# Other sums for feed forward's seven products, other places for the last parts of the output projection, and own banks for transposes in a two-layer decoder kernel

## The chip, the core and the metric

The kernel runs on one core of a Trainium2 chip. The core has five engines with an instruction queue each: TensorE (PE in the profile, with its weight loads as PEld), VectorE (DVE), ScalarE (ACT), GpSimd (POOL) and SyncE (SP), which issues the DMAs here. The metric is the device time of one execution in microseconds (us). Data lies in SBUF; PE writes into eight PSUM banks, each of which holds a 128x512 float32 tile.

## What is computed

Two layers, each with three kinds of attention beside each other and a feed forward part, on 1024 tokens of 1024 columns. The change touches the end of the output projection and the feed forward part:

```
for layer in range(DEPTH):            # DEPTH = 2
    ...                               # h = rmsnorm(x, ln1_g), three mixers
    mixed = jnp.concatenate([out_a, out_b, out_c], axis=-1)
    x = x + mixed @ w_o[layer]
    u = rmsnorm(x, ln2_g[layer]) @ w_up[layer]          # 1024 -> 4096
    x = x + jnp.square(jax.nn.relu(u)) @ w_down[layer]  # 4096 -> 1024
return rmsnorm(x, final_g)
```

## The kernel before

Every product of 128x128 by 128x512 is three matmuls: each operand is split into a high part, rounded to PE's format, and a low part, the remainder; high by high, high by low and low by high are summed in one bank (`mm3`, line 500). So each operand costs a rounding (`copy` with the kind "fhi", on ACT or POOL) and a subtraction (`pair` with "flo", on DVE or POOL).

The two matrices of feed forward are multiplied by a scheme of seven products instead of eight: tokens, inner columns and outer columns are each halved, and each of the seven products takes a sum or difference of quarters from the left and one from the right. Before, the tables `left` and `right` (line 1313 on) hold these sums, five of the seven a side being real ones (`parts`, line 1320); each product's result is then added to several quarters of the output.

Up (1024 to 4096) runs over 16 pairs `p` of column blocks. `up_a` (line 1435) does products 4 and 2, which need the first half of the tokens alone; `up_b_` (line 1447) the other five. `up_load` fetches the weights `wu`, `up_parts` makes the weights' sums `s_wu` and their high and low parts `uh`, `ul` in 16 slots of the tag "w". A pair uses four banks (products 4 and 2 share one, 5 and 3, 1 and 7, and 6); ACT copies a bank's first result away (`fsnap`) before the second product is added to it. `relu2` makes the squared ReLU. The quarters and their sums `hc` go to DRAM for down. Five pairs' `up_a` run ahead (`AHEAD`).

The normed tokens come from four steps `tp` of two token tiles each: ACT squares a tile with a sum (`jk_u`), DVE takes the root by Newton steps (`rv`, `ra`, `usq`), ACT and POOL scale the tile (`fnorm`), PE transposes it into a bank (`ptu`, from the same eight-deep tag "u" that up's products use), and ACT and DVE bring it to SBUF with the gain (`xq`). `x_parts` makes the tokens' sums `s_x` and their parts `xc`.

Down (4096 to 1024) runs in four blocks of pairs (`BLOCKS`), in each over the seven products in `ORDER` and four token tiles. `ha` are the parts of the tokens' side, `hb` of the weights'; results go to five accumulators `acc` and to the residual `xd`, and after the last block 32 additions a layer combine the accumulators into the residual. The last pair is done plainly (`pdl`, with `hpa` and `hpb`).

The output projection adds four groups of two column blocks to x (`project`, line 1193). The last two groups, (2, 3) and (4, 5), run after attention; the last one's parts are popped from the list `bl`, four at each step `tp`.

All operations are first recorded and then issued in an order that a planner works out: it walks over all engines with a table of costs and hops, takes on each engine the ready operation with the lowest rank (program position plus `nc.bias`), and picks the engine where `WAYS` leaves a choice. Each engine then runs its row strictly in that order. All instructions carry the line of the helper that issues them (L416), so places are told by tiles.

## Time and profile before

| | |
|---|---|
| time, median of 3 runs | 2592.06 us (2591.5 to 2594.74) |
| the profiled execution | 2590.82 us, span 2589.0 us |
| mean granted clock of PE | 0.983 of full speed |
| PE busy | 2479.6 us (96%), 12808 matmuls and transposes |
| DVE, ACT, POOL busy | 2146.6 (83%), 1265.7 (49%), 935.9 us (36%) |
| DMA | 360.61 MB, mean 139 GB/s |

PE's busy time is a share of a span that has very different stages; a busy PE may also run at half its clock. So the stages are read apart, by the table of stretches, which gives busy time, number of instructions, granted clock and DMA share of each. In the first layer the feed forward part starts near 622 us, up's steady pace is between 740 and 960, down ends near 1300; in the second the same places lie near 1903, 2020 to 2240 and 2560.

### The profile page before, as it was taken

To read this page: it belongs to the slowest core of one execution; us is meant where nothing else is said; L and a number is where in the kernel's file an instruction comes from. 1 tells how busy PE (TensorE), PEld (TensorE's weight loads), DVE (VectorE), ACT (ScalarE), POOL (GpSimd) and SP (SyncE) were. 2 spreads that over 40 slices of the span, in tenths; PEclk is the share of its full clock that TensorE was granted. 3 is DMA by queue.
4 is the path that set the end of the run, shared out by engine and by line. 5 is a ranking of instruction groups with operands and counts; after the bars stand their busy time and mean duration, and the time that the engine had idled before them with its cause. 6 is when DMAs were issued, how large, how long until landed. Compare 5 with 4: busy or idle time off the path is not lost.

```text
span 2589.0 us, 39628 instructions
## 1 busy us (share of the span) xinstructions
PE 2479.6 (96%) x12808; PEld 2085.7 (81%) x12808; DVE 2146.6 (83%) x4489; ACT 1265.7 (49%) x2626; POOL 935.9 (36%) x1093
## 2 busy tenths in 40 slices
PE   9999999998899999999899999999979999999996
PEld 7777889987688878888688778898867888788884
DVE  4688988888888778899856799978889887789999
ACT  3566667734544444233235666777255444442332
POOL 1344355644100013336624344557431000133374
PEclk9999999999999999999999999999989999999998
DMA  8355434523344467444353454344324454765332
GB/s 253 100 133 137 122 83 108 149 76 122 97 164 162 155 213 262 130 148 122 122 164 98 131 137 118 82 115 142 93 85 141 148 179 137 279 199 162 119 98 85
DMA packets 292639, 360.61 MB, mean 139 GB/s; under 512 B 48848, under 2 KB 172112, under 8 KB 292432
## 3 DMA queue, kind: packets, MB, share of 16 engines
q1 hardware_dynamic: 292432, 358.08, 45.0%
q8 instruction: 102, 1.67, 0.3%
q14 instruction: 105, 0.86, 0.1%
HBM read 231.63 MB, written 94.90 MB: 126 GB/s over the span
## 4 chain that ended last, share of the span: by engine, by line
PE 74%; DVE 13%; DMA 5%; issue 3%; ACT 2%; POOL 2%; SPq 1%; DVEq 0%; POOLq 0%; ACTq 0%
PE pu L416 21%; PE pd L416 16%; PE po L416 5%; PE pf_C L416 5%; PE pf_A L416 4%; PE s_B L416 3%; PE pj L416 2%; PE o_B L416 2%; PE o_A L416 2%; DVE hb L416 2%; PE ptp_A L416 2%; PE ptp_B L416 2%; PE s_A L416 2%; DVE xd L416 1%; DVE p_C L416 1%
## 5 line engine op out<-in xcount | busy, mean ns | idle before, releaser
L416 PE MATMUL pd<-hb,ha 128*128 128x512 f32 x2520 | 578.7, 391 | 7.6 <-DVE hb L416 5.7
L416 PEld LDWEIGHTS pd<-hb,ha 128*128 128x128 f32 x2520 | 474.2, 189 | 111.1 <-DVE hb L416 9.7
L416 PE MATMUL pu<-xc,uh 128*128 128x512 f32 x1792 | 550.8, 391 | 6.5 <-ACT s L416 3.4
L416 PEld LDWEIGHTS pu<-xc,uh 128*128 128x128 f32 x1792 | 334.3, 188 | 83.8 <-ACT s L416 10.9
L416 PE MATMUL pu<-xc,ul 128*128 128x512 f32 x896 | 344.3, 390 | 0.8 <-DVE ul L416 0.8
L416 ACT ACTIVATE hb<-s_wd 128x512 fp32r<-128x512 f32 x135 | 83.9, 628 | 241.4 <-DVE s_wd L416 112.6
L416 PEld LDWEIGHTS pu<-xc,ul 128*128 128x128 f32 x896 | 168.2, 188 | 37.2 <-DVE ul L416 1.7
L416 DVE TENSOR_TENSOR ha<-hr,ha 128x512 fp32r<-128x512 f32 x164 | 148.0, 905 | 38.7 <-POOL ha L416 30.2
L416 ACT ACTIVATE uh<-s_wu 128x512 fp32r<-128x512 f32 x124 | 77.6, 631 | 204.1 <-PE pu L416 172.4
L416 POOL TENSOR_SCALAR ha<-hr 128x512 fp32r<-128x512 f32 x88 | 76.3, 870 | 228.7 <-DVE acc L416 89.3
L416 POOL TENSOR_SCALAR uh<-s_wu 128x512 fp32r<-128x512 f32 x36 | 31.0, 862 | 323.6 <-DVE ul L416 191.2
L416 DVE TENSOR_TENSOR ul<-s_wu,uh 128x512 fp32r<-128x512 f32 x160 | 109.9, 690 | 42.8 <-ACT uh L416 42.2
L416 DVE TENSOR_TENSOR hb<-s_wd,hb 128x512 fp32r<-128x512 f32 x135 | 136.9, 1030 | 0.8 <-ACT hb L416 0.6
L416 ACT ACTIVATE p_C<-p_C,w_C 128x256 f32<-128x256 f32 (+7 forms) x128 | 98.9, 773 | 54.3 <-DVE w_C L416 53.7
L416 DVE TENSOR_TENSOR s_wu<-wu,wu 128x512 f32<-128x512 f32 x160 | 108.9, 692 | 13.9 <-DMA wu<-in_w_up_dram 8.2
L416 POOL TENSOR_SCALAR p_A<-p_A,w_A 128x128 f32<-128x128 f32 (+3 forms) x96 | 76.9, 803 | 116.6 <-DVE w_A L416 83.3
L416 DVE TENSOR_TENSOR xr<-po,xr 128x512 f32<-128x512 f32 x128 | 86.5, 683 | 31.8 <-PE po L416 31.4
L416 DVE TENSOR_TENSOR s_wd<-wd,wd 128x512 f32<-128x512 f32 x142 | 100.8, 740 | 7.3 <-DMA wd<-in_w_down_dram 7.3
L416 PE MATMUL pf_C<-wh_C,hh 128*128 128x512 f32 x256 | 104.5, 412 | 1.3 <-ACT cqj L416 0.9
L416 PE MATMUL pf_C<-wl_C,hh 128*128 128x512 f32 x256 | 104.3, 407 | 1.3 <-DVE wl_C L416 1.0
L416 PE MATMUL po<-h_wo,mixh 128*128 128x512 f32 x256 | 102.9, 402 | 0.1
L416 PE MATMUL pf_A<-wh_A,hh 128*128 128x512 f32 (+1 forms) x256 | 100.1, 395 | 2.7 <-POOL wh_A L416 1.6
(344 smaller groups left out, 6771.4 us busy)
## 6 DMA issues: line engine op xcount, KB each, us to landing
hr<-hc_dram SPq DMA_DIRECT2D x210, 256.0 KB, 2.8
hc_dram<-hc SPq DMA_DIRECT2D x150, 256.0 KB, 3.0
...
wd<-in_w_down_dram SPq DMA_DIRECT2D x120, 256.0 KB, 4.6
...
```

The costliest lines, as they stand in the source:

```text
L416: getattr(getattr(self.nc, eng), method)(*[real(v) for v in args], **{k: real(v) for k, v in kw.items()})
```

## The change

The four parts of the change in words:

- Feed forward takes another form of the seven products, with four sums a side, where each sum is built on the one before. In up, products 1 and 2 share a bank, 5 and 3 share one, 6, 7 and 4 a third; what stands in a bank is added by DVE to the outputs before the next product goes into the same bank. In down the products run in the order 6, 5, 7, 4, 3, 1, 2; three accumulators stay, products 7, 4, 3 and 2 are added straight to the residual, and the combination (20 additions a layer) follows product 1 of the last block.
- The output projection's last group has three column blocks and one: tokens 0 to 511 get three blocks into eight banks and then the last one; the rest follows tile by tile between the norms (`project_rest`).
- The transposes have a tag of banks of their own ("t", four deep).
- The second half of the tokens goes from PSUM straight into the sums (`xt`), the first half through `xq` as before.

Its core:

```diff
-BANKS = {'s': 6, 'pt': 3, 'o': 2, 'x': 3, 'c': 6, 'l': 4, 'v': 3, 'f': 5, 'j': 8, 'u': 8, 'd': 8}
+BANKS = {'s': 6, 'pt': 3, 'o': 2, 'x': 3, 'c': 6, 'l': 4, 'v': 3, 'f': 5, 'j': 8, 'u': 8, 't': 4, 'd': 8}
...
-ORDER = (5, 4, 3, 2, 1, 6, 7)
+ORDER = (6, 5, 7, 4, 3, 1, 2)
...
-XB = (150, 100, -40)
+XB = -40
 NB = (0, 0)
-XR = 4
+XR = 1
...
-        groups = [(6, 0), (7, 1), (2, 3), (4, 5)]
+        groups = [(6, 0), (7, 1), (2, 3, 4), (5,)]
...
+        most, last = project_load(2), project_load(3)
+        po_ = {}
+        for t in range(4):
+            for c in range(2):
+                po_[t, c] = bank("d", f"po_{L}_2_{t}_{c}")
+                project_mm(po_[t, c], t, c, *most, True, False)
+        for t in range(4):
+            for c in range(2):
+                project_mm(po_[t, c], t, c, *last, False, True)
+                project_add(po_[t, c], t, c)
+        def project_rest(t):
+            for c in range(2):
+                o = bank("d", f"po_{L}_2_{t}_{c}")
+                project_mm(o, t, c, *most, True, False)
+                project_mm(o, t, c, *last, False, True)
+                project_add(o, t, c)
...
+        def up_sum(p, i, a, b, op):
+            v = tl("tmp", [P, 4, P], f"su_{L}_{p}_{i}")
+            pair("fadd", v, a, b, op)
+            return v
...
+            if tp > 1:
+                project_rest(2 * tp)
+                project_rest(2 * tp + 1)
...
-                pt = bank("u", f"ptu_{L}_{tp}_{k}")
+                pt = bank("t", f"ptu_{L}_{tp}_{k}")
...
+                    for d in range(2):
+                        copy("fevac", xq[k][d][:, cs], p_[d], g_[d])
+                    for d in range(2):
+                        x_parts(1 + d, k, cs, xq[k][d][:, cs])
+                else:
+                    q = tl("tmp", [P, 2, 256], f"xt_{L}_{tp}_{k}")
+                    r = tl("tmp", [P, 256], f"xt2_{L}_{tp}_{k}")
+                    b11, b21 = [xq[k][d][:, cs] for d in range(2)]
+                    nc.vector.scalar_tensor_tensor(q[:, 0], p_[0], g_[0], b11, ALU.mult, ALU.subtract)
+                    b22 = x_tile_of(3, k)
+                    nc.scalar.activation(b22[:, 0, cs], p_[1], AF.Copy, scale=g_[1])
+                    nc.vector.scalar_tensor_tensor(b22[:, 1, cs], p_[1], g_[1], b22[:, 0, cs].bitcast(F32), ALU.mult, ALU.subtract)
+                    x_parts(5, k, cs, q[:, 0])
+                    nc.vector.scalar_tensor_tensor(r, p_[1], g_[1], q[:, 0], ALU.mult, ALU.subtract)
+                    x_parts(6, k, cs, r)
+                    pair("fadd", q[:, 1], r, b11, ALU.subtract)
+                    x_parts(7, k, cs, q[:, 1])
+                    pair("fadd", r, b21, r, ALU.subtract)
+                    x_parts(4, k, cs, r)
...
+        def plus(o, ps, v):
+            nc.vector.tensor_tensor(out=o, in0=ps, in1=v, op=ALU.add)
...
         def up_a(p):
...
+                up_load(p, (0,) if p < AHEAD else (0, 1))
+            for d in range(2):
+                up_parts(p, 1 + d, up_w[p, 0, d])
+            o = bank("u", f"pu_{L}_{p}_1")
+            up_mm(p, 1, o, True)
+            copy("fsnap", e[:, 0], o)
+            up_mm(p, 2, o, False)
+            relu2(e[:, 1], o)
...
+            a11, a12, a21, a22 = [up_w[p, f, d] for f in range(2) for d in range(2)]
+            s1 = up_sum(p, 1, a21, a22, ALU.add)
+            up_parts(p, 5, s1)
+            s2 = up_sum(p, 2, s1, a11, ALU.subtract)
+            up_parts(p, 6, s2)
+            pair("fadd", s2, a12, s2, ALU.subtract)
+            up_parts(p, 3, s2)
+            s3 = up_sum(p, 3, a11, a21, ALU.subtract)
+            up_parts(p, 7, s3)
+            up_parts(p, 4, a22)
+            h12, h22 = [tl("pp", [P, 512], f"h{z}_{L}_{p}") for z in (12, 22)]
+            z_ = bank("u", f"pu_{L}_{p}_5")
+            up_mm(p, 5, z_, True)
+            plus(h22, z_, m1)
+            up_mm(p, 3, z_, False)
+            plus(h12, z_, m1)
+            y = bank("u", f"pu_{L}_{p}_6")
+            up_mm(p, 6, y, True)
+            plus(h12, y, h12)
+            relu2(h12, h12)
+            up_mm(p, 7, y, False)
+            plus(h22, y, h22)
+            relu2(h22, h22)
+            up_mm(p, 4, y, False)
+            plus(m1, y, m1)
+            relu2(m1, m1)
...
+            pair("fadd", c1, b21, b22, ALU.add)
+            keep(5, c1)
+            pair("fadd", c2, c1, b11, ALU.subtract)
+            keep(6, c2)
+            pair("fadd", c3, b11, b21, ALU.subtract)
+            keep(7, c3)
+            c4 = tl("pp", [P, 512], f"hc_{L}_{p}_3")
+            pair("fadd", c4, b12, c2, ALU.subtract)
+            keep(3, c4)
...
+        acc = {i: [tl("stk", [P, 2, 512], f"acc_{L}_{i}_{h}") for h in range(2)] for i in (6, 5, 1)}
...
+                    if i == 6:
+                        dn_t[p] = tl(TT[p - b0], [P, 2, 512], f"wt_{L}_{p}")
+                    if i in (4, 5, 6, 7):
+                        t3, t2 = dn_t[p][:, 0], dn_t[p][:, 1]
+                    if i == 6:
+                        pair("fadd", t3, b22, b12, ALU.subtract)
+                        pair("fadd", t2, t3, b11, ALU.add)
+                    if i == 4:
+                        pair("fadd", t2, b21, t2, ALU.subtract)
+                    t1 = None
+                    if i == 5:
+                        t1 = tl("tmp", [P, 512], f"wt1_{L}_{p}")
+                        pair("fadd", t1, b12, b11, ALU.subtract)
+                    hi_lo(b[:, 0], b[:, 1], {1: b11, 2: b21, 3: b22, 5: t1}[i] if i in (1, 2, 3, 5) else t3 if i == 7 else t2)
...
+                    if i in (6, 5, 1):
+                        to = acc[i][t // 2][:, t % 2]
                     else:
-                        to = acc[i][t // 2][:, t % 2]
-                    if first and i < 6:
+                        to = {7: xs[t + 4][:, 512:], 4: xs[t + 4][:, 0:512], 3: xs[t][:, 512:], 2: xs[t][:, 0:512]}[i]
+                    if first and i in (6, 5, 1):
                         copy("fsnap", to, o)
                     else:
-                        nc.vector.tensor_tensor(out=to, in0=o, in1=to, op=ALU.add)
+                        plus(to, o, to)
+                    if b1 == BLOCKS[-1] and i == 1:
+                        a6, a5, a1 = [acc[z][t // 2][:, t % 2] for z in (6, 5, 1)]
+                        pair("fadd", xs[t + 4][:, 0:512], xs[t + 4][:, 0:512], a1, ALU.add)
+                        pair("fadd", a5, a5, a1, ALU.add)
+                        pair("fadd", xs[t + 4][:, 512:], xs[t + 4][:, 512:], a5, ALU.add)
+                        pair("fadd", a1, a1, a6, ALU.add)
+                        pair("fadd", xs[t][:, 512:], xs[t][:, 512:], a1, ALU.add)
```

What it moves is shown at three places; `before` has L416 and the change L418 in its rows, and the last number of a name tells copies of a tile apart.

PE's row in layer 1 from the last parts of the output projection (`po`) to up's first products (`pu`), before; `ptu_1` is the transposes of step 1, `pu_0_4` product 4 of pair 0:

```order
L416 MATMUL po_3_4_0_8073<-h_wo_5_0_7869,mixl_5_7886 128x512
L416 MATMUL ptu_0_0_8082<-ident,xr_0_6513 128x128 x4
...
L416 MATMUL ptu_0_3_8103<-ident,xr_0_6513 128x128 x4
L416 MATMUL po_3_4_1_8111<-h_wo_4_1_7835,mixh_4_7807 128x512
...
L416 MATMUL po_3_7_1_8228<-h_wo_5_1_7888,mixl_5_7886 128x512
L416 MATMUL ptu_1_0_8267<-ident,xr_0_6513 128x128
...
L416 MATMUL ptu_1_3_8289<-ident,xr_3_6805 128x128
L416 MATMUL ptu_2_0_8296<-ident,xr_3_6805 128x128
...
L416 MATMUL ptu_2_3_8307<-ident,xr_3_6805 128x128 x3
L416 MATMUL ptu_3_0_8417<-ident,xr_6_5223 128x128
...
L416 MATMUL ptu_3_3_8441<-ident,xr_7_5231 128x128
L416 MATMUL pu_0_4_8449<-xc_4_0_8123,uh_0_4_7947 128x512 x2
```

The same place after the change:

```order
L418 MATMUL po_2_4_1_7994<-h_wo_3_1_7619,mixl_3_7803 128x512
L418 MATMUL ptu_0_0_8002<-ident,xr_0_6505 128x128 x4
...
L418 MATMUL ptu_1_3_8119<-ident,xr_3_6775 128x128
L418 MATMUL po_2_5_1_8090<-h_wo_3_1_7619,mixl_3_7803 128x512
...
L418 MATMUL po_2_7_0_8194<-h_wo_5_0_7854,mixl_5_7852 128x512
L418 MATMUL ptu_2_0_8221<-ident,xr_3_6775 128x128
...
L418 MATMUL po_2_7_1_8236<-h_wo_5_1_7869,mixl_5_7852 128x512
L418 MATMUL pu_0_1_8287<-xc_1_0_8027,uh_0_1_8200 128x512 x2
...
L418 MATMUL pu_4_1_8476<-xc_1_0_8027,uh_4_1_8339 128x512
L418 MATMUL ptu_3_0_8505<-ident,xr_6_5223 128x128
...
L418 MATMUL pu_4_1_8476<-xc_2_3_8071,ul_4_2_8375 128x512
L418 MATMUL pu_0_5_8647<-xc_5_0_8277,uh_0_5_8641 128x512 x2
```

Steps 1, 2 and 3 stood together behind the last `po`; now `po` matmuls stand ahead of steps 0 to 2, and the products of up that need only the first tokens ahead of step 3.

PE's row in up at pair 8, before, from product 5 to product 3 in the bank `pu_8_5`:

```order
L416 MATMUL pu_8_5_9992<-xc_5_3_8359,ul_8_5_9859 128x512
L416 MATMUL pu_8_1_10045<-xc_1_0_8381,uh_8_1_9904 128x512 x2
L416 MATMUL pu_8_1_10045<-xc_1_0_8381,ul_8_1_9911 128x512
L416 MATMUL pu_8_1_10045<-xc_1_1_8386,uh_8_1_9904 128x512 x2
L416 MATMUL pu_8_1_10045<-xc_1_1_8386,ul_8_1_9911 128x512
L416 MATMUL pu_8_5_9992<-xc_3_0_8630,uh_8_3_9870 128x512 x2
```

After the change, from product 5 to 3, and around product 7 in the bank `pu_8_6`:

```order
L418 MATMUL pu_8_5_9877<-xc_5_3_8451,ul_8_5_9724 128x512
L418 MATMUL pu_8_6_9901<-xc_6_8314,uh_8_6_9734 128x512 x2
L418 MATMUL pu_8_6_9901<-xc_6_8314,ul_8_6_9744 128x512
L418 MATMUL pu_8_6_9901<-xc_6_8314,uh_8_6_9734 128x512 x2
L418 MATMUL pu_8_5_9877<-xc_3_0_8275,uh_8_3_9764 128x512 x2
...
L418 MATMUL pu_10_1_9941<-xc_1_2_8058,uh_10_1_9823 128x512
L418 MATMUL pu_8_6_9901<-xc_7_8332,uh_8_7_9777 128x512 x2
...
L418 MATMUL pu_8_6_9901<-xc_7_3_8535,ul_8_7_9789 128x512
L418 MATMUL pu_10_1_9941<-xc_1_2_8058,uh_10_1_9823 128x512
L418 MATMUL pu_10_1_9941<-xc_1_2_8058,ul_10_1_9836 128x512
L418 MATMUL pu_10_1_9941<-xc_1_3_8068,uh_10_1_9823 128x512 x2
L418 MATMUL pu_10_1_9941<-xc_1_3_8068,ul_10_1_9836 128x512
L418 MATMUL pu_8_6_9901<-xc_4_0_8361,uh_8_4_9812 128x512 x2
```

DVE's row there, with the additions that read the banks between the products:

```order
L418 TENSOR_TENSOR h_0_8_9903<-pu_8_5_9877,ua_8_9643 128x512
L418 TENSOR_TENSOR ul_9_6_9908<-su_9_2_9781,uh_9_6_9899 128x512
L418 TENSOR_TENSOR su_9_2_9781<-wu_9_1_0_9603,su_9_2_9781 128x512
L418 TENSOR_TENSOR h_0_8_9929<-pu_8_5_9877,ua_8_9643 128x512
L418 TENSOR_TENSOR ul_9_3_9934<-su_9_2_9781,uh_9_3_9926 128x512
L418 TENSOR_TENSOR su_10_2_9943<-su_10_1_9891,wu_10_0_0_9651 128x512
L418 TENSOR_TENSOR h_0_8_9929<-pu_8_6_9901,h_0_8_9929 128x512
L418 TENSOR_TENSOR ul_9_7_9951<-su_9_3_9795,uh_9_7_9939 128x512
L418 TENSOR_TENSOR su_10_3_9957<-wu_10_0_0_9651,wu_10_0_1_9656 128x512
L418 TENSOR_TENSOR h_0_8_9903<-pu_8_6_9901,h_0_8_9903 128x512
```

Between two products in one bank five matmuls of the other bank or of pair 10 stand now, and the reader is a DVE addition (`h_0_8<-pu_8_5`) among sums and low parts; before, six stood there and ACT read the bank.

POOL's row at the end of down in layer 1, before; `xd` is the residual, `acc_3_0` an accumulator's tile:

```order
L416 TENSOR_TENSOR hb_14_2_13544<-wd_14_0_0_13136,hb_14_2_13544 128x512
L416 TENSOR_TENSOR s_wd_14_1_13572<-wd_14_0_0_13136,wd_14_1_1_13152 128x512
L416 TENSOR_TENSOR xd_0_11270<-xd_0_11270,acc_3_0_11586 128x512 x2
L416 TENSOR_TENSOR acc_4_1_11514<-acc_4_1_11514,acc_5_1_11398 128x512
L416 TENSOR_TENSOR hb_14_1_13617<-s_wd_14_1_13572,hb_14_1_13617 128x512
L416 TENSOR_TENSOR s_wd_12_6_13644<-wd_12_0_0_12381,wd_12_0_1_12385 128x512
L416 TENSOR_TENSOR xd_3_11352<-xd_3_11352,acc_2_0_11672 128x512
L416 TENSOR_TENSOR acc_3_0_11586<-acc_3_0_11586,acc_2_0_11672 128x512
L416 TENSOR_TENSOR xd_3_11352<-xd_3_11352,acc_2_0_11672 128x512
```

And after the change, from the last tokens' parts on:

```order
L418 TENSOR_SCALAR ha_13_2_13444<-hr_13_2_13348 128x512
L418 TENSOR_SCALAR hpa_30_13465<-hpr_30_0_13392 128x512
L418 TENSOR_TENSOR acc_1_0_11642<-acc_1_0_11642,acc_6_0_11213 128x512
L418 TENSOR_SCALAR wh_0_13506<-wr_0_13481,g_518 128x512
L418 TENSOR_TENSOR hpb_30_13515<-hpr_30_0_13392,hpa_30_13465 128x512
L418 TENSOR_TENSOR hpb_31_13527<-hpr_31_0_13428,hpa_31_13517 128x512
L418 TENSOR_TENSOR hpb_30_13515<-hpr_30_1_13415,hpa_30_13465 128x512
L418 TENSOR_TENSOR hpb_31_13527<-hpr_31_1_13460,hpa_31_13517 128x512
L418 TENSOR_TENSOR acc_1_1_11683<-acc_1_1_11683,acc_6_1_11226 128x512 x2
```

The additions that combine accumulators stood in a row on POOL; now three are left there, and the low parts `hpb` of the last pair, which were DVE's, stand between them.

## Rows read from the trace of the kernel before

**Rows 1.** The page: busy time of each engine, its share of the span, instructions.

```profile
PE 2479.6 (96%) x12808; PEld 2085.7 (81%) x12808; DVE 2146.6 (83%) x4489; ACT 1265.7 (49%) x2626; POOL 935.9 (36%) x1093
```

**Rows 2.** Stretches (us from the span's start): length, busy time (instructions), clock, DMA.

```profile
622.00:660.00 38.00, 22.05 (x109) 19.38 (x109) 31.03 (x97) 25.02 (x54) 18.47 (x26) 0.73 0.20 77
660.00:700.00 40.00, 38.13 (x166) 30.67 (x165) 34.92 (x64) 25.69 (x52) 6.34 (x8) 1.00 0.32 93
740.00:960.00 220.00, 218.78 (x961) 179.26 (x960) 179.03 (x279) 102.84 (x182) 18.34 (x22) 1.00 0.50 167
960.00:985.00 25.00, 24.55 (x107) 19.67 (x106) 16.33 (x26) 8.57 (x16) 4.97 (x6) 1.00 1.00 366
1220.00:1270.00 50.00, 42.37 (x176) 33.57 (x174) 48.99 (x51) 11.72 (x21) 47.30 (x29) 0.97 0.23 69
1270.00:1302.00 32.00, 29.78 (x153) 25.41 (x153) 24.98 (x39) 14.42 (x28) 6.01 (x7) 0.89 0.67 237
1903.00:1940.00 37.00, 21.07 (x104) 18.49 (x103) 30.38 (x97) 24.86 (x53) 18.28 (x26) 0.72 0.19 75
2500.00:2550.00 50.00, 41.34 (x172) 32.73 (x170) 49.04 (x52) 11.72 (x21) 45.07 (x28) 0.94 0.19 58
1272.00:1278.00 6.00, 5.78 (x15) 4.55 (x16) 5.48 (x10) 0.73 (x1) 1.57 (x2) 0.54 0.71 187
```

**Rows 3.** Chain that ended last: start, length in us, instructions without a wait.

```profile
983.55 181.71 PE pd L416 x799
1295.16 7.10 PE ptx L416 x64
```

**Rows 4.** In order of time, projection's end, layer 1: start, length; brackets: idle, releaser.

```profile
614.79 0.39 PE L416 MATMUL po<-h_wo,mixl 128*128 128x512 f32 x1
615.22 0.69 DVE L416 TENSOR_TENSOR xr<-po,xr 128x512 f32<-128x512 f32 x1 [0.63 <-PE po L416]
621.82 2.08 PE L416 MATMUL ptu<-ident,xr 128*128 128x128 f32 x16
637.44 6.21 PE L416 MATMUL ptu<-ident,xr 128*128 128x128 f32 x32 [4.00 <-POOL xr L416]
654.93 0.47 PE L416 MATMUL ptu<-ident,xr 128*128 128x128 f32 x1 [11.28 <-ACT xr L416]
```

**Rows 5.** In order of time at the end of down, layer 1, DVE and PE.

```profile
1271.48 0.68 DVE L416 TENSOR_TENSOR hpb<-hpr,hpa 128x512 fp32r<-128x512 f32 x1
1272.22 0.80 PE L416 MATMUL pdl<-h_wd,hpb 128*128 128x512 f32 x1 [6.34 <-DVE hpb L416]
```

**Rows 6.** Groups of DVE, 640 to 740: busy us, mean ns, idle before.

```profile
L416 DVE TENSOR_TENSOR xc<-s_x,xc 128x256 fp32r<-128x256 f32 x22 | 10.6, 510 | 1.6 <-ACT xc L416 1.1 <-POOL xc L416 0.3
L416 DVE TENSOR_TENSOR s_x<-xq,xq 128x256 f32<-128x256 f32 x19 | 7.3, 416 | 0.0
L416 DVE TENSOR_SCALAR xq<-ptu,g 128x256 f32<-128x256 f32 x9 | 4.0, 479 | 4.1 <-PE ptu L416 4.1
```

**Rows 7.** Groups of POOL and DVE in down's last block, 1210 to 1270.

```profile
L416 POOL TENSOR_TENSOR xd<-xd,acc 128x512 f32<-128x512 f32 x11 | 18.5, 1698 | 0.0
L416 POOL TENSOR_TENSOR acc<-acc,acc 128x512 f32<-128x512 f32 x11 | 17.7, 1616 | 1.9 <-DVE acc L416 1.8
L416 DVE TENSOR_TENSOR ha<-hr,ha 128x512 fp32r<-128x512 f32 x13 | 15.9, 1230 | 0.0
L416 DVE TENSOR_TENSOR hb<-s_wd,hb 128x512 fp32r<-128x512 f32 x10 | 14.4, 1442 | 0.0
L416 DVE TENSOR_TENSOR acc<-pd,acc 128x512 f32<-128x512 f32 x17 | 11.5, 680 | 0.9 <-PE pd L416 0.9
```

**Rows 8.** Groups of PE and ACT, 740 to 960, then DVE's wait there (total, times, longest).

```profile
L416 PE MATMUL pu<-xc,uh 128*128 128x512 f32 x641 | 196.8, 390 | 1.2 <-ACT s L416 1.2
L416 ACT ACTIVATE s<-pu 128x512 f32<-128x512 f32 x24 | 14.0, 585 | 5.7 <-DMA hc_dram<-hc 2.3 <-DVE hc L416 1.6 <-DVE ul L416 1.0
DVE ul L416 <- ACT uh L416: 18.2, 15, 2.6
```

More of the change, by code (lines that the diff above doesn't have):

```diff
@@ new lines, in project_mm, with project_add @@
+        def project_mm(o, t, c, ws, mx, start, stop):
+            ts_ = slice(t * P, (t + 1) * P)
+            for fi in range(len(mx)):
+                mm3(o, mx[fi][0][:, ts_], mx[fi][1][:, ts_], ws[fi][c][0], ws[fi][c][1], start and fi == 0, stop and fi == len(mx) - 1)
+        def project_add(o, t, c):
+            cs = slice(c * 512, (c + 1) * 512)
+            nc.vector.tensor_tensor(out=xs[t][:, cs], in0=o, in1=xs[t][:, cs], op=ALU.add)
+        def project(gi):
+            box = []
+            def part(t, c):
+                o = bank("f", f"po_{L}_{gi}_{t}_{c}")
+                project_mm(o, t, c, *box[0], True, True)
+                project_add(o, t, c)
+            return [(0, lambda: box.append(project_load(gi)))] + [(1296, lambda t=t, c=c: part(t, c)) for t in range(NT) for c in range(2)]
@@ L1408, in tile_trunk, with up_mm @@
[L1408 to L1424 removed]
+        def up_mm(p, i, o, start):
+            wh, wl = up_h[p, i]
+            for k in range(4):
+                mm3(o, wh[:, k], wl[:, k], xc[i, k][:, 0], xc[i, k][:, 1], start and k == 0, k == 3)
@@ L1465, in up_b_ @@
[L1465 to L1480 removed]
+                up_load(p, (0, 1))
@@ L1513, in dn_load @@
                     dn_w[p, f, z] = q
+        TT = ("stk", "stk", "stk", "hs")
         for b0, b1 in zip(BLOCKS, BLOCKS[1:]):
+            dn_t = {}
             for p in range(b0, b1):
```

241 lines of the change are left out of this document (81 added, 160 removed).

## The prediction, made before the changed kernel ran

> **What bounds the kernel now.** I read the engines' busy times first: TensorE (PE) is busy for 2479.6 of 2589.0 us [rows 1], so no engine has to get faster; some 109 us of idle PE, and the time at a low granted clock, are all that can be won. Next I read the stretches [rows 2] against a pitch. In a long chain without waits 799 matmuls of 128x512 take 181.71 us, 0.2275 each; 64 transposes take 7.10, 0.111 each [rows 3]. With these, a stretch's loss is its length less its PE instructions at those prices:
> - 622 to 660 (end of output projection, norms, start of up): 64 transposes (7.1), 45 matmuls (10.2), so 38.0 - 17.3 = 20.7 lost, at clock 0.73. Then 660 to 700: 40 - 166 x 0.2275 = 2.2. Layer 2 has the same place at 1903: 104 instructions, about 20.8 lost.
> - 740 to 960 (up at its steady pace): 220 - 961 x 0.2275 = 1.4, clock 1.00.
> - 1220 to 1270 (last block of down): 50 - 176 x 0.2275 = 10.0; 1270 to 1302 loses 4.6 more (64 transposes, 89 matmuls), 2500 to 2550 in layer 2 10.9.
> So three places a layer matter. Last I read those in order of time. At the first [rows 4] PE does its 42 remaining projection matmuls, then has nothing but 48 transposes: it waits 4.00 us for x normed by GpSimd (POOL) and 11.28 us for ScalarE (ACT), because each pair of tiles needs its square, a Newton root and a scaling one after another; the second transposes run slowly, 32 in 6.21 us. At the end of down PE waits 6.34 us for `hpb` [rows 5], a VectorE (DVE) subtraction queued behind the final combination.
>
> **The change part by part.** PE's work is equal: as many matmuls and transposes, same shapes. So each term is a change of loss.
>
> *Output projection's last parts.* The merged groups give tokens 0 to 511 first; 24 short matmuls finish them, and what remains for tokens 512 to 1023 (96 matmuls, 21.8 us, against 42 before) stands between the transposes. Let T0 be the end of those 24. From the start of a tile's second addition to the first transpose the chain of before took 621.82 - 615.22 = 6.6 us [rows 4]. Tile 1's second addition starts at about T0 - 2.5, so `ptu_0` can start at T0 + 4.1; PE comes to it after 18 matmuls, T0 + 4.1. `ptu_1` follows 16 transposes (1.8) and 23 matmuls (5.2) later, T0 + 11.1; its chain, behind the first on ACT and DVE, I put at T0 + 10.4. `ptu_2` comes after 43 more matmuls, T0 + 22.7, and its tiles' last addition at T0 + 15 plus 6.6 lies before. PE leaves the projection at T1 = T0 + 27.2, with products 1 and 2 of up ready, which need the first tokens alone.
>
> *The second half's parts.* PE now has five pairs' products 1 and 2 (120 matmuls, 27.3 us) to cover norms and sums of tokens 512 to 1023. On DVE each pair of tiles costs about 12 subtractions straight from PSUM, 25 additions of 128x256 and 2 of 128x512. No such subtraction is in the trace; the nearest row is the scaling from PSUM at 0.479, the upper bound for one more SBUF operand is the 128x256 pair at 0.510 [rows 6]. I take 0.46 as the step from one to the next, 0.35 for additions (0.416 long, and records overlap by 0.07), 0.60 for the long ones: 5.5 + 8.8 + 1.2 = 15.5 us. `ptu_3` starts at T1 + 19.6 (86 matmuls), first parts at T1 + 20.3, and product 5 of the first pair, whose weights' low part is the last in that DVE row, is ready at T1 + 35.8. PE has run out at T1 + 29.1 (1.8 of transposes, 34 matmuls): a stall of some 6.5 us. After 6.34 us of idle before, 15 matmuls took 6 us at clock 0.54 [rows 2], 2.6 over their pitch; I add that. With 1.5 for small waits the place loses 10.6 instead of 22.9: **gain 12.3 a layer**. Bounds: no stall but 4 of small waits, 19; DVE at 1.5 times these prices (it ran `hb` at 1.442 instead of 0.68 beside POOL's additions [rows 7]), 15 us more of stall over both tile pairs, a loss of 3. I lean to the cheap end, since POOL has no additions here but low parts of x.
> [...]
>
> *Up's four sums.* A pair has 20 DVE instructions instead of 23, and three ACT copies fewer: off PE's path at both ends, worth nothing there. But the order puts products into one bank: 5 then 3, and 6, 7, 4, with one DVE addition that must read the bank in between, and 5, 7 and 5 other matmuls as cover. Before, ACT copies of 0.585 us did this under 5 or 6 matmuls and PE lost 1.2 us to them in 220 [rows 8]. The price of the new hop: a projection matmul that starts at 614.79 lets the addition start at 615.22 [rows 4, 5], 0.43 later; a DVE operation that starts at 1271.48 lets PE start at 1272.22 [rows 5], 0.74. So 1.17 us after the last matmul's start, against 6 x 0.2275 = 1.37 when PE comes back: 0.2 to spare, if DVE is free. It is in use for 20 x 0.6 = 12 of 19 us a pair, and is in order. With 48 such additions a layer, one in four late by 0.2 us: **-2.4 a layer**, bounds 0 and -10.
>
> *Into down.* The first block starts with product 6, which needs two sums and three loads of weights a pair. The stretch 960 to 985 moves 366 GB/s with all DMA queues' share at 1.00 and loses 0.7 [rows 2]; loads stand in it before too. **-1.5 a layer**, bounds 0 and -5.
>
> *End of down.* Before, 32 additions a layer combine the accumulators after the last product; 22 run on POOL at 1.6 to 1.7 us and slow DVE's SBUF pairs to 1.230 and 1.442, while additions from PSUM stay at 0.680 [rows 7]. Now 20 remain, placed behind product 1 with product 2 (36 matmuls, 8.2 us) and the last parts as cover; 3 are on POOL; `hpb` is POOL's and its order has it 12 us of matmuls ahead of its use. DVE's last block has about 90 rows at 0.62, 56 us, beside 252 matmuls, 57.3: close, so I leave 5 of the 14.6 lost: **gain 9.5 in layer 1, 8.5 in layer 2**, bounds 4 and 12.
>
> *Sum.* 2 x (12.3 - 2.4 - 1.5) + 9.5 + 8.5 = 34.8. The profiled execution took 2590.82; the median of the three runs is 1.2 higher, so I take off 34.8 from 2592.06: **2557**. The last norm and output, after all matmuls, are unchanged.
>
> **The rivals.**
> *The bank hop stalls PE* (slower). If DVE waits behind a low part whose high part ACT delivers late, the freeing addition queued behind it is late too. Such waits exist: 18.2 us, 15 times, longest 2.6, in 220 us [rows 8]; against it, PE felt none of them there, and DVE now has fewer rows. At 0.5 us on each of 48 additions in two layers it is 48 us in place of my 4.8: 2592 - 34.8 + 43 = 2600. It turns the sign from 0.41 us an addition.
> [...]
> *Second half late.* DVE's two times 15.5 us run at contended prices: a stall of 14 instead of 6.5, and 5 instead of 2.4 a layer in up: 2557 + 15 + 5 = 2577.
> *The wait only moves* (no change). The stall before product 5 grows to 17 and down's end stays bound by DVE (gain 4 a layer instead of 9): 34.8 - 2 x 10.5 - 10 = 4 us faster, 2588.
>
> **How the numbers follow.** Forecast 0.65 (2538 to 2572), second half late 0.11 (2572 to 2586), only moves 0.09, bank hop 0.11, clock 0.04. About 0.2%, 5 us, is what a measurement of this kernel can tell from no change. So faster 0.76, same 0.09, slower 0.15. The range takes in the forecast's own bounds, the two weaker cases and the cheap half of the bank hop: 2536 to 2598.
>
> **What would show it.** In the changed kernel's profile: PE's transposes of the second, third and fourth pair of tiles without waits of 4 and 11 us, and one wait of 5 to 9 us before the product with `xc_5`, released by DVE; in up, PE's waits for the DVE additions `h` below 5 us a layer with clock 1.00; at the end of down no wait of 6 us for `hpb`, and DVE's pairs near 0.7 instead of 1.2 to 1.4. I am wrong if waits of PE on `h<-pu` sum to 20 us a layer, or if the wait before product 5 is over 15.

## The result, and the profile after

The changed kernel takes 2549.16 us (median of four runs, 2548.45 to 2549.46), the kernel before beside it 2592.56. The ratio is 0.9831, 95% interval 0.9814 to 0.9848: 43.4 us faster, inside the range and 8 us beyond the forecast of 2557. The profiled execution has a span of 2547.7 against 2589.0, 41.3 us less.

PE does the same 12808 instructions; DVE has 163 fewer than in [rows 1], from the page:

```profile
PE 2473.8 (97%) x12808; PEld 2077.0 (82%) x12808; DVE 2069.9 (81%) x4326; ACT 1238.3 (49%) x2548; POOL 920.2 (36%) x1078
```

The stretches of the changed kernel (from the span's start: length, then busy time and instructions of PE, PEld, DVE, ACT, POOL, then clock, DMA share, GB/s):

```profile
610.00:740.00 130.00, 123.26 (x557) 100.18 (x556) 113.33 (x250) 72.06 (x136) 22.82 (x31) 0.97 0.44 144
740.00:960.00 220.00, 219.01 (x963) 179.57 (x962) 166.26 (x248) 97.25 (x160) 17.89 (x19) 1.00 0.51 172
960.00:985.00 25.00, 23.09 (x100) 18.07 (x99) 20.63 (x22) 12.28 (x23) 12.77 (x10) 1.00 1.04 365
1220.00:1270.00 50.00, 49.98 (x220) 40.81 (x219) 45.29 (x64) 13.19 (x23) 18.64 (x15) 1.00 0.40 128
1860.00:1980.00 120.00, 113.26 (x512) 92.04 (x512) 100.48 (x230) 64.96 (x124) 22.31 (x30) 0.97 0.39 130
2460.00:2527.80 67.80, 67.80 (x300) 55.91 (x299) 61.20 (x119) 17.78 (x30) 20.35 (x17) 1.00 0.21 66
```

And three of the kernel before that hold the same work, wide enough that all 64 transposes lie in the first two:

```profile
610.00:740.00 130.00, 111.96 (x498) 91.81 (x497) 111.68 (x243) 69.80 (x136) 29.41 (x38) 0.92 0.38 125
1900.00:2020.00 120.00, 102.33 (x457) 83.91 (x457) 103.94 (x222) 67.38 (x131) 29.64 (x38) 0.91 0.37 121
2460.00:2573.00 113.00, 102.95 (x436) 83.25 (x435) 110.49 (x168) 33.31 (x57) 74.17 (x52) 0.95 0.25 78
```

With the prediction's two prices (0.2275 us a matmul, 7.1 us for the 64 transposes) each length less its instructions is a loss. The junction from projection to up loses 130 - 493 x 0.2275 - 7.1 = 10.7 us in layer 1, where it lost 24.2; in layer 2 11.0 against 23.5. The end of down lost 14.6 in layer 1 [rows 2] and 13.8 in layer 2 (the row from 2460 to 2573); now both lose nothing. Up loses 0.9 instead of 1.4 [rows 2], the start of down 2.2 instead of 0.7.

That is 54.4 us gained at four places. Two places give some of it back. The last matmul starts at 2573.06 before and at 2527.86 after, 45.2 us earlier, but the span ends only 41.3 earlier: the tail grew by 3.9. And 5.4 us were lost ahead of the two projections, at places whose code the change does not touch (the first projection starts at 523.7 instead of 520.2; from the second layer's first transposes to its projection it is 1.9 longer). With some 3 lost at the start of down and 1 gained in up: 54.4 - 3 + 1 - 3.9 - 5.4 = 43, against 41.3 seen; a few missing matmul records can make the difference.

Inside the junction, PE's longer waits in order of time (start, length; in brackets idle and releaser), to be read against [rows 4]:

```profile
667.50 0.73 PE L418 MATMUL pu<-xc,uh 128*128 128x512 f32 x2 [2.25 <-ACT ua L418]
672.37 0.73 PE L418 MATMUL pu<-xc,uh 128*128 128x512 f32 x2 [1.83 <-ACT ua L418]
674.13 1.06 PE L418 MATMUL pu<-xc,uh 128*128 128x512 f32 x2
679.12 0.71 PE L418 MATMUL pu<-xc,uh 128*128 128x512 f32 x2 [2.22 <-issue]
682.49 1.05 PE L418 MATMUL pu<-xc,uh 128*128 128x512 f32 x2
```

No transpose waits 4 or 11 us any more. Three waits of 6.3 us together are left; for the third the profile names no releaser ("issue"). Between 673.7 and 683.5 rows of two matmuls take up to 1.06 instead of 0.62, because the granted clock falls twice to 0.50 of full speed: some 1.2 us after the second wait has ended, and 1.3 us after the third. Between the two it is at 1.00 (three stretches; the third number from the end is the clock):

```profile
673.60:676.90 3.30, 3.30 (x8) 2.01 (x7) 3.17 (x8) 0.83 (x2) 0.55 (x2) 0.50 0.00 0
677.00:680.30 3.30, 1.18 (x4) 0.75 (x5) 1.67 (x4) 1.99 (x4) 0.26 (x1) 1.00 0.21 79
680.40:683.70 3.30, 3.30 (x9) 2.61 (x8) 2.16 (x5) 1.05 (x2) 0.00 (x0) 0.50 0.14 37
```

Seven matmuls before the third wait go at some 0.43 us, twelve after it take 4.65, together 3.3 us more than their pitch. 6.3 + 3.3 leaves 1.1 of small waits in 10.7.

The first two waits are for `ua`, ACT's copy of a bank between products 1 and 2 (of pairs 3 and 4). ACT's row shows what the first copy waits for in turn:

```profile
664.66 1.27 ACT L418 ACTIVATE xc<-xt 128x256 fp32r<-128x256 f32 x3 [1.36 <-DVE xt L418]
666.85 0.60 ACT L418 ACTIVATE ua<-pu 128x512 f32<-128x512 f32 x1 [0.92 <-DVE xt L418]
```

DVE's sums `xt` of the second half release it. The code has a reason: the tiles `ua` of pairs 3 and 4 have the tag "pw", whose five slots are held by two tiles `xq` and three `xc`, so a copy can be written only when DVE has read an `xq` for the last time. That this is the reason is read from the code and this row; no run tried it.

### The profile page after: what moved, and what is told of

Read it like the earlier page. It is cut to its first block, busy times and chain, and to the rows that moved or that the text cites. A ratio compares the mean times of both kernels' runs of the same rounds, so it can differ in the third digit from the quotient of the medians.

```text
span 2547.7 us, 39227 instructions
## 1 busy us (share of the span) xinstructions
PE 2473.8 (97%) x12808; PEld 2077.0 (82%) x12808; DVE 2069.9 (81%) x4326; ACT 1238.3 (49%) x2548; POOL 920.2 (36%) x1078
## 5 line engine op out<-in xcount | busy, mean ns | idle before, releaser
L418 PE MATMUL pd<-hb,ha 128*128 128x512 f32 x2520 | 577.2, 390 | 5.4 <-DVE hb L418 3.5
L418 PE MATMUL pu<-xc,uh 128*128 128x512 f32 x1792 | 552.7, 393 | 13.4 <-ACT ua L418 8.2
L418 PEld LDWEIGHTS pd<-hb,ha 128*128 128x128 f32 x2520 | 471.4, 188 | 109.6 <-DVE hb L418 8.3
L418 PEld LDWEIGHTS pu<-xc,uh 128*128 128x128 f32 x1792 | 336.9, 189 | 90.0 <-ACT ua L418 10.0
L418 PE MATMUL pu<-xc,ul 128*128 128x512 f32 x896 | 346.7, 393 | 0.0
L418 PEld LDWEIGHTS pu<-xc,ul 128*128 128x128 f32 x896 | 169.6, 189 | 36.8 <-DVE ul L418 0.8
L418 DVE TENSOR_TENSOR ha<-hr,ha 128x512 fp32r<-128x512 f32 x151 | 145.6, 967 | 24.8 <-POOL ha L418 23.0
L418 POOL TENSOR_SCALAR ha<-hr 128x512 fp32r<-128x512 f32 x90 | 74.1, 824 | 245.1 <-DVE xd L418 94.8
L418 ACT ACTIVATE hb<-wt 128x512 fp32r<-128x512 f32 x98 | 60.4, 627 | 184.4 <-PE pd L418 157.3
L418 ACT ACTIVATE uh<-su 128x512 fp32r<-128x512 f32 x124 | 77.5, 631 | 138.4 <-PE pu L418 121.6
L418 ACT ACTIVATE hb<-wd 128x512 fp32r<-128x512 f32 x82 | 50.4, 627 | 158.8 <-PE pd L418 157.3
L418 ACT ACTIVATE p_C<-p_C,w_C 128x256 f32<-128x256 f32 (+7 forms) x128 | 98.9, 773 | 55.3 <-DVE w_C L418 54.7
L418 POOL TENSOR_SCALAR p_A<-p_A,w_A 128x128 f32<-128x128 f32 (+3 forms) x96 | 77.2, 806 | 116.5 <-DVE w_A L418 83.6
L418 POOL TENSOR_SCALAR uh<-wu 128x512 fp32r<-128x512 f32 x16 | 13.3, 832 | 280.1 <-PE pu L418 168.5
L418 DVE TENSOR_TENSOR hb<-wt,hb 128x512 fp32r<-128x512 f32 x105 | 109.7, 1061 | 0.7 <-ACT hb L418 0.5
L418 DVE TENSOR_TENSOR xd<-pd,xd 128x512 f32<-128x512 f32 x128 | 86.8, 682 | 26.6 <-PE pd L418 26.5
L418 PE MATMUL pf_C<-wh_C,hh 128*128 128x512 f32 x256 | 104.7, 413 | 1.7 <-POOL wh_C L418 0.9
L418 PE MATMUL pf_C<-wl_C,hh 128*128 128x512 f32 x256 | 104.4, 408 | 0.4 <-DVE wl_C L418 0.3
L418 PE MATMUL po<-h_wo,mixh 128*128 128x512 f32 x256 | 103.3, 403 | 1.0 <-POOL h_wo L418 1.0
L418 POOL TENSOR_SCALAR p_B<-p_B,w_B 128x384 f32<-128x384 f32 (+4 forms) x96 | 74.4, 780 | 79.8 <-DVE w_B L418 62.3
L418 PE MATMUL pf_A<-wh_A,hh 128*128 128x512 f32 (+1 forms) x256 | 100.0, 395 | 3.0 <-DVE w_C L418 2.1
L418 PE MATMUL pf_C<-wh_C,hs_C 128*128 128x512 f32 x256 | 101.8, 401 | 0.7 <-DMA hs_C<-hl_dram 0.7
```

Of the source, the lines that this page charges most:

```text
L418: getattr(getattr(self.nc, eng), method)(*[real(v) for v in args], **{k: real(v) for k, v in kw.items()})
```

## The experiments

Each ran beside the kernel before (2591.3 to 2593.7 us in these sessions). "Saved" is one less the ratio, times 2592.

### Is it the projection's matmuls between the norms that cover them?

The prediction said so. Two runs: the changed kernel with those matmuls all ahead of the first norm, and the kernel before with the new projection alone.

```diff
-            if tp > 1:
-                project_rest(2 * tp)
-                project_rest(2 * tp + 1)
+            if tp == 0:
+                for t in range(4, NT):
+                    project_rest(t)
```

> The changed kernel with one part undone: the last parts of the output projection for tokens 512 to 1023 all stand ahead of the first norm instead of between the norms; sums, banks and down as in the changed kernel. Theory (the matmuls between the norms cover the norm chains): PE then waits again for the scaled tiles of the second to fourth step; the 72 matmuls between steps are 16 us of cover, and products 1 and 2 of up can still cover the last two steps, so 8 to 16 us a layer come back: 2565 to 2581 us. Rival (the gain at this place comes from the new up form, whose first products need only the first tokens, and the place of the projection is indifferent): within 3 us of 2549.

Measured: 2548.57 us, ratio 0.9837 (0.9822 to 0.9851), the same as the changed kernel, as the rival had it. Its junction has the same 557 instructions in 130 us.

The second run takes the changed `project_load`, `project_mm`, `project_add` and `project_rest` into the kernel before and nothing else.

> The kernel before with one part of the change alone: the groups (2, 3, 4) and (5) of the output projection, tokens 0 to 511 first and the rest between the norms; feed forward as before. Theory (cover between the norms is the main part of the gain at this place): of 23 us lost there a layer at least 10 go, 2565 to 2575 us. Rival (without the direct parts of the second half DVE is late with the sums and PE waits the same time a little later): 2583 to 2593 us.

Measured: 2599.41 us, 1.0028 (1.0016 to 1.0039), slower, outside both ranges. PE's waits there (total, times, longest):

```profile
PE ptu L418 <- POOL xr L418: 42.7, 2, 21.3
```

So with the matmuls that were to be the cover in their new places, PE still waits 21.3 us a layer, now in one piece before the last pair of tiles; and without them between the norms nothing is lost. The cover is something else.

### Own banks: alone, left out, and with the rest

Left out (the changed kernel with the transposes back in up's tag):

```diff
-                pt = bank("t", f"ptu_{L}_{tp}_{k}")
+                pt = bank("u", f"ptu_{L}_{tp}_{k}")
```

> The changed kernel with the transposes of the normed tokens in the banks' tag of up's products again, as before the change. Theory (the banks' tag alone is worth little; the tags share the same eight banks): within 5 us of 2549. Rival (transposes of the last step wait in the tag's turn behind products 1 of the five pairs): 5 to 15 us slower a layer.

Measured: 2565.24 us, 0.9897 (0.9881 to 0.9913): 17 us of the 44 are gone, 8.5 a layer, as the rival had it in size. The order of the wait is the reverse of the rival's.

```profile
PE ptu L418 <- ACT xr L418: 34.6, 4, 17.0
```

Banks of a tag are handed out in program order. With one tag, up's first product cannot get a bank until all 16 transposes' banks have been taken, so PE must reach the last pair of tiles before it may start up, and waits 17.0 us a layer for its norm. With an own tag products 1 and 2 of five pairs stand before the last transposes and are the cover. The forecast had counted on them as cover for the last step, but not on the banks that allow it.

Then the tag alone was put into the kernel before (the reverse of the two lines of the change), then with the new down, then with the new down and the new projection, which is all of the change but the new up.

> The kernel before with one thing of the change: the transposes of the normed tokens take banks of their own tag instead of up's. Theory A: the tag is what opens the junction, because up's first products can now start before the last pair of tiles is normed. The junction then loses about 11 instead of 23 us a layer (the wait of 11 us before the third transposes becomes cover by products 4 and 2 of up, the 4 us before the second stay): 2567 us, 2562 to 2572. Theory B: the tag pays only together with the merged projection groups and the four sums, which bring the first tokens earlier: 2583 to 2592.

> The kernel before with its own banks for the normed tokens' transposes and the new down, but with the old sums of up and the old projection. Theory A: the two parts add up, 2564.5 less 24: 2541 us, 2537 to 2547, so the rest of the change (four sums, second half straight from PSUM, merged projection) is worth nothing or costs some us, and this version is faster than the changed kernel. Theory B: the new up and projection carry some of the gain: 2550 us or more.

> The same with the new projection added: all of the change but the new sums of up. Theory A: as the one without the new projection within 3 us, since the place of the projection's matmuls decided nothing once before: 2538 to 2547. Theory B: the four sums are needed, and without them this is slower than the changed kernel, 2552 to 2560.

| | us | ratio (95%) |
|---|---|---|
| tag alone | 2601.99 | 1.0035 (1.0023 to 1.0048) |
| new down alone | 2564.49 | 0.9895 (0.9880 to 0.9910) |
| new down, tag | 2562.90 | 0.9884 (0.9871 to 0.9898) |
| new down, tag, new projection | 2568.16 | 0.9905 (0.9891 to 0.9918) |
| the whole change less the tag | 2565.24 | 0.9897 (0.9881 to 0.9913) |
| the whole change | 2549.16 | 0.9831 (0.9814 to 0.9848) |

My theory A, that the tag by itself opens the junction, fell, and the tag alone is slower than theory B's range too. In the two runs that add the new down and the new projection theory A fell as well: they are 16 and 21 us above its ranges. In the kernel before the tag does what it says (up starts at 642.6 instead of 659.2), and the 11.28 us of [rows 4] are gone, but the time is not won. PE in order of time, tag alone:

```profile
637.79 5.10 PE L416 MATMUL ptu<-ident,xr 128*128 128x128 f32 x32 [4.01 <-POOL xr L416]
656.25 1.97 PE L416 MATMUL ptu<-ident,xr 128*128 128x128 f32 x16 [1.19 <-POOL xr L416]
675.91 1.22 PE L416 MATMUL pu<-xc,uh 128*128 128x512 f32 x2 [4.29 <-ACT ua L416]
685.26 1.83 PE L416 MATMUL pu<-xc,uh 128*128 128x512 f32 x3 [3.87 <-ACT uh L416]
```

The waits moved behind the first products: one for ACT's copy `ua` of a bank, one for the weights of product 5. The stretch 610 to 740 holds 503 instructions, a loss of 23.0 against 24.2. In up, 740 to 960, the order that came with it loses 8.2 us (931 instructions instead of 961), 5.3 of them in four waits for ACT's copies `s`, where 1.4 were lost, so the tag alone is slower. With the new down as well the second wait is 6.50, and the three queues show where it is from:

```profile
685.97 1.84 PE L416 MATMUL pu<-xc,uh 128*128 128x512 f32 x3 [6.50 <-ACT uh L416]
684.55 1.90 DVE L416 TENSOR_TENSOR s_wu<-wu,wu 128x512 f32<-128x512 f32 x3 [2.55 <-DMA wu<-in_w_up_dram]
681.22 16.56 SPq L416 DMA_DIRECT2D wu<-in_w_up_dram  x10
```

PE waits for the high part of a sum of weights, DVE's sum for its load, and the load is issued at 681.22. In the code of before the normed second half (`xq`, `k` 2 and 3) lies in the slots "p2" and "oo", which product 5's weights need next; DVE starts the last sum that reads `xq` at 679.00. The new up takes the second half straight from PSUM, has no such tile, and builds that sum at 675.76. With the new projection too, a wait of 7.51 us for `xc` stands before up's first product, which in the old form is product 4 and needs a difference of tokens; the new form begins with products 1 and 2, which need none. So the new up is worth 19 us beside the tag, and the tag 17 beside the new up. Without the new up the tag saves 2 or 3 us beside the new down, less than the intervals tell apart, and costs some 9 in the kernel before. That slots and sum-free first products are what the new up brings is read from these rows and the code; the two were not tried apart.

### The end of down

New down alone in the kernel before:

> The kernel before with the down part of the change alone. Theory (parts add up): as far under the kernel before as the changed kernel with old down is over the changed kernel, 2564 to 2572 us. Rival (down's gain needs the lighter up): above 2580.

Measured: 2564.49 us, 27 us saved, where the forecast's terms for the end of down were 18. The number lies in the theory's range, but the theory's premise does not hold: the changed kernel with the old down, below, is 110 us slower, for another reason. Is it the fewer and earlier additions, or that POOL no longer does them? Two runs: the kernel before with its 32 additions a layer on DVE alone, and the changed kernel with its 20 after product 2 instead of product 1.

```diff
-            pair("fadd", a4, a4, a5, ALU.subtract)
+            dve_pair(a4, a4, a5, ALU.subtract)
...
+        def dve_pair(o, a, b, op):
+            nc.vector.tensor_tensor(out=o, in0=a, in1=b, op=op)
```

> The kernel before with the 32 additions of the combination a layer on DVE alone, none on GpSimd. Theory B (contention: GpSimd's additions stretch DVE's pairs from 0.68 to 1.2 to 1.7 us, so taking 22 of them off GpSimd costs DVE 13 us and gives it back some 20): faster than before by 5 to 15 us, 2577 to 2587. Theory A (DVE has too many rows in the last block, whoever else runs): slower than before by 10 to 20 us, 2602 to 2612.

Measured: 2580.91 us, 0.9960 (0.9947 to 0.9973): 10 us faster, as theory B had it, with 22 additions a layer more on the engine that was 98% busy there. Its groups of DVE, 1210 to 1270 (busy us, mean ns, idle before), to be read against [rows 7]:

```profile
L416 DVE TENSOR_TENSOR acc<-pd,acc 128x512 f32<-128x512 f32 x17 | 11.5, 679 | 0.0
L416 DVE TENSOR_TENSOR ha<-hr,ha 128x512 fp32r<-128x512 f32 x13 | 11.2, 865 | 0.0
L416 DVE TENSOR_TENSOR hb<-s_wd,hb 128x512 fp32r<-128x512 f32 x11 | 10.6, 961 | 0.0
```

`ha` falls from 1230 to 865 ns and `hb` from 1442 to 961, the additions from PSUM stay at 0.68. The means of [rows 7] mix: in the kernel before most single instructions of these groups take 0.68, about 1.18 or about 1.77 us (`ha` at 1236.82 0.68 and at 1224.31 1.18, `hb` at 1233.93 1.77), so most were either not held or held by some 0.5 or 1.1 us. The stretches at the end of down in this run:

```profile
1220.00:1270.00 50.00, 48.72 (x214) 39.90 (x213) 50.00 (x71) 8.48 (x15) 26.99 (x21) 1.00 0.31 90
1270.00:1302.00 32.00, 27.46 (x146) 23.56 (x147) 30.63 (x49) 17.02 (x32) 2.77 (x4) 0.95 0.76 269
```

The second holds the 64 transposes, so by the two prices they lose 1.3 and 6.2, together 7.5 where 14.6 were lost: half is gained. The last matmul starts at 2561.0 of 2580.8, so the tail has grown to 19.8 here too; two times 7 less 3.9 is the 10 measured. In the changed kernel the stretch 1210 to 1270 reads:

```profile
L418 DVE TENSOR_TENSOR ha<-hr,ha 128x512 fp32r<-128x512 f32 x10 | 6.9, 687 | 2.1 <-POOL ha L418 2.1
L418 DVE TENSOR_TENSOR hb<-wd,hb 128x512 fp32r<-128x512 f32 x9 | 6.2, 683 | 0.0
L418 POOL TENSOR_TENSOR acc<-acc,acc 128x512 f32<-128x512 f32 x3 | 3.9, 1290 | 8.1 <-DVE acc L418 8.1
```

> The changed kernel with the 20 additions that combine the accumulators behind product 2, after all products, instead of behind product 1. Theory A (the gain at the end of down is that few additions are left and that they run early, under product 2's matmuls): PE or the last norms wait again, 4 to 8 us a layer, 2557 to 2565 us. Theory B (the gain is that GpSimd's additions are gone, which stretched DVE's, and the place matters little): within 3 us of 2549.

Measured: 2549.4 us, 0.9835 (0.9817 to 0.9854), as theory B had it: the place of the additions is worth nothing. So half of what the end of down gained is DVE's speed without a row of POOL additions beside it. The other half is not shown by a run of its own. The new down has 12 additions a layer less; at 0.68 us each they are an estimated 8 us of DVE, near the 7.5 that were left.

The reverse, the changed kernel with the old down, told nothing on this:

> The changed kernel with the down part of the kernel before (its sums, its order of products, five accumulators and 32 additions behind the last product). Theory (down's part is worth some 14 us a layer, 28 in all less 4 us that the last norms give back): 2570 to 2578 us, with the wait for the last pair's low part back at the end of down. Rival (the wait at the end of down depends on what the layer brings along, not on down's form): under 2560.

Measured: 2659.72 us, 1.0264. The old down wants five sums of up's outputs for each pair, and with the new up these share the five slots "pp" with its outputs, so up itself slowed: PE waited 45.8 us for `h` and `uh`. Of its rows only the last is of use, the wait for `hpb` of [rows 5], which is back at 6.4 us a layer:

```profile
PE pu L418 <- DVE h L418: 23.1, 23, 2.6
PE pu L418 <- ACT uh L418: 22.7, 46, 0.5
PE pdl L418 <- DVE hpb L418: 12.8, 2, 6.4
```

### The price of a bank's return

The forecast charged 1.17 us from the last matmul into a bank to the next product in it. To see that price the planner of the changed kernel was told that PE learns 0.46 us earlier of DVE's reads of up's banks, so that it puts only three other matmuls between most such products instead of five to seven.

```diff
-                at[u] = max(at[u], end + HOPS.get((e, next(iter(ops[u].ways))), HOP[e]))
+                at[u] = max(at[u], end - (soon_ if "tensor" in ops[u].ways else 0.0) + HOPS.get((e, next(iter(ops[u].ways))), HOP[e]))
```

> The changed kernel, planned as if PE learned 0.46 us earlier that DVE has read a bank of up, so that 44 products return to their bank after 3 other matmuls and 16 after 4, instead of 5 and 7. Prediction's price of a return, 1.17 us from the start of the last matmul: 44 x (1.17 - 0.91) + 16 x 0.03 = 12 us of waits of PE on DVE's additions, 2559 to 2565 us. Rival (the return is much cheaper, or DVE's row is so late that every return was near a wait already): under 2553, or over 2575.

Measured: 2577.45 us, 0.9943 (0.9922 to 0.9963): 28 us slower than the changed kernel, over twice the 12 expected. Three stretches of up in this run, and one return, DVE and PE in order of time:

```profile
740.00:960.00 220.00, 216.91 (x916) 168.78 (x915) 154.40 (x221) 98.45 (x164) 22.81 (x18) 1.00 0.45 152
690.00:950.00 260.00, 256.50 (x1084) 199.69 (x1083) 190.25 (x277) 118.15 (x197) 22.82 (x18) 1.00 0.48 159
1965.00:2225.00 260.00, 256.50 (x1084) 199.62 (x1083) 190.40 (x279) 118.33 (x198) 22.63 (x18) 1.00 0.47 159
```

```profile
811.88 0.39 PE L420 MATMUL pu<-xc,ul 128*128 128x512 f32 x1
812.11 0.62 PE L420 MATMUL pu<-xc,uh 128*128 128x512 f32 x2
812.30 0.69 DVE L420 TENSOR_TENSOR h<-pu,h 128x512 f32<-128x512 f32 x1
812.56 0.39 PE L420 MATMUL pu<-xc,ul 128*128 128x512 f32 x1
813.05 0.73 PE L420 MATMUL pu<-xc,uh 128*128 128x512 f32 x2
813.62 0.40 PE L420 MATMUL pu<-xc,ul 128*128 128x512 f32 x1
```

The bank's last matmul starts at 811.88, DVE's addition at 812.30 (0.42 later), PE comes back at 813.05 (0.75 after that): 1.17, the forecast's 0.43 + 0.74. Four slots of 0.2275 are 0.91, so PE waits 0.26. But the two matmuls that follow take 0.57 instead of 0.455: a restart costs 0.11 more. At 0.38 a return, up to three returns a pair and some 11 pairs are 12.5 us at most; the first stretch loses 11.6, in the changed kernel 0.9. The two longer ones, one in each layer, lose 13.4 each, in the changed kernel nothing (1144 and 1143 instructions in 260 us of up): 27 of the 28 us. That is some 35 returns a layer at 0.38, 70 in all, where the expectation had 44 at 0.26; both the number of waiting returns and the price of one were too low. The total lies in the rival's "over 2575", but not for the rival's reason, since DVE's row is not late. The clock is 1.00 in these stretches, so waits of 0.26 us, some 35 a layer, did not lower it.

### The tail

In the changed kernel DVE is busy for all of the stretch in which PE ends, and beside its last norms POOL multiplies three of the eight tiles by the gain:

```profile
2500.00:2520.00 20.00, 20.00 (x89) 16.32 (x88) 20.00 (x42) 3.85 (x7) 6.22 (x5) 1.00 0.00 1
L418 POOL TENSOR_TENSOR y<-y,gf 128x512 f32<-128x512 f32 x6 | 8.9, 1502 | 18.4 <-ACT y L418 18.4
```

(a stretch, and a group of POOL, 2500 to 2550). The last run puts these on DVE too:

```diff
-LN = (0, 2, 4)
+LN = ()
```

> The changed kernel, but in the last norms VectorE also multiplies tiles 0, 2 and 4 by the gain, so that GpSimd does nothing there. Theory A: GpSimd's six multiplications stretch VectorE's rows by more than they save, since VectorE is the bound of the tail: 1 to 3 us faster, 2546 to 2548. Theory B: VectorE is bound by its own work, and six more rows of 0.6 to 0.7 us make it 4 us slower, 2553.

Measured: 2545.7 us (2544.45 to 2547.22), 0.9817 (0.9804 to 0.9831), as theory A had it and 0.3 below its range, the fastest of all kernels here, 3.5 us below the changed kernel by medians of two sessions; the intervals of the two ratios overlap, so the profile decides. Groups of DVE, 2500 to 2550, first of the changed kernel:

```profile
L418 DVE SCALAR_TENSOR_TENSOR y<-xd,fsq,gf 128x512 f32<-128x512 f32 x10 | 9.1, 955 | 0.0
L418 DVE SCALAR_TENSOR_TENSOR ra<-fsq,rh 128x1 f32<-128x1 f32 x24 | 7.7, 340 | 0.1
```

and without POOL's part:

```profile
L418 DVE SCALAR_TENSOR_TENSOR y<-xd,fsq,gf 128x512 f32<-128x512 f32 x16 | 11.3, 747 | 0.0
L418 DVE SCALAR_TENSOR_TENSOR ra<-fsq,rh 128x1 f32<-128x1 f32 x24 | 4.5, 214 | 0.0
```

Six more instructions cost 2.2 us, and the one-column steps alone give back 3.2. The means hide how. In the changed kernel 21 of the 24 steps `ra` take 0.21 or 0.22 us as without POOL, and three take over 1.2, each beside a multiplication of POOL. One of each, and POOL's pair beside the first:

```profile
2522.17 2.98 POOL L418 TENSOR_TENSOR y<-y,gf 128x512 f32<-128x512 f32 x2 [11.08 <-ACT y L418]
2523.93 1.24 DVE L418 SCALAR_TENSOR_TENSOR ra<-fsq,rh 128x1 f32<-128x1 f32 x1
2525.88 0.21 DVE L418 SCALAR_TENSOR_TENSOR ra<-fsq,rh 128x1 f32<-128x1 f32 x1
```

With one step `fsq` of 1.19 us instead of 0.15 and two `y` of about 1.8 instead of 0.75, six instructions of DVE are held by some 1.0 us each: as many as POOL has multiplications there.

From the last matmul's start (2528.58) to the end it takes 16.8 us, in the changed kernel 19.8, before 15.9: 3.0 of the 3.9 come back. The other runs bear this out: it is 19.1 to 19.9 in all that have the new down or the combination on DVE, 15.8 to 16.0 in those with the old one on POOL.

## Why the prediction held, and which of its steps did not

- **In sum, partly luck.** The forecast is 8 us off because two errors met: its terms for feed forward were too small by 17.6 us (below), and 9.3 us were lost at places for which it had no term.
- **Junction: right in size, wrong in cause.** Gain forecast 12.3 a layer, measured 13.5 and 12.5; loss forecast 10.6, of it 6.5 stall, 2.6 slow clock, 1.5 small; measured 10.7 of 6.3, 3.3 and 1.1. But the step "what remains for tokens 512 to 1023 stands between the transposes" was named as the cover and is worth nothing (2548.57), and the own banks, which got no price at all, carry 17 us beside the new up. The order shown ahead of the prediction had products 1 and 2 before the last transposes; what allowed it was not asked. That the size came out is luck for this step. The cover named for the last step, products 1 and 2, is the one that holds.
- **The one stall before product 5.** Forecast 6.5, released by DVE. Of the 6.3 only the last 2.2 is at product 5, and no releaser is named for it; 4.1 is PE waiting for ACT's copy `ua` of pairs 3 and 4, whose first one waits for DVE's sums. So DVE's second half is behind this stall too, but one product earlier and through ACT: the forecast had not asked what else on ACT hangs on that row of DVE. The forecast's prices on DVE were near: operations straight from PSUM took 0.474 to 0.478, and a step of 0.40 from one to the next where 0.46 was taken.
- **Up.** Forecast -2.4 a layer, measured +0.5 in layer 1. The price of 1.17 was exact; "one in four late by 0.2 us" was not needed, since the planner kept five to seven other matmuls between (PE waits 0.8 us for `h<-pu` in the whole run, far from the 20 that would have proved me wrong). The rival of the bank hop needed 0.41 us an addition; the run that forced the hop reached 0.38 a return. The clock, to which the forecast gave 0.04, was 1.00 from 740 to 960, in that run too; where it fell, to 0.50 in the junction, the waits ahead were of about 2 us.
- **Into down.** Forecast -1.5, measured -1.5 in layer 1.
- **End of down: the mis-sized term.** Forecast 9.5 and 8.5, measured 14.6 and 13.8. I left 5 of the loss because DVE's last block had "about 90 rows at 0.62, 56 us" beside 57 us of matmuls. DVE is busy for 45.3 of 50 us there, PE never waits, and nothing of the loss is left.
- **Last norm "unchanged".** It is 3.9 longer. When down's end no longer waits, DVE is the bound there (busy for 28.00 of the 28.00 us from 2500 to 2528) and has more left to do after the last matmul. POOL's multiplications stood there before too (six, from 2560.4 on), but now each instruction of DVE that they hold counts: without them 3.0 of the 3.9 come back.
- **Ahead of the projections.** 5.4 us longer at places whose code the change does not touch. The 3.5 in layer 1 lie within the spread from execution to execution: the last run has the same code there and starts the projection at 520.3, not 523.7, and all 14 profiles put it between 517.8 and 523.7 (519.0 to 523.7 with the new up, 517.8 to 522.5 without). In layer 2 the 1.9 are not: from the first transposes to the projection the seven profiles with the new up take 507.1 to 511.8 us, the seven without it 503.2 to 505.9. So the new up costs between 1.2 and 8.6 us there; why is open.

In sum feed forward gave some 52 us where 34.8 was forecast (down's end 10 more, up 6 more, the rest small), and 9 of them went at places that had no term.
